# A hybrid decoder layer on one core: root steps and products of some recurrent heads moved from GpSimd to VectorE

## The chip, the core and the metric

The kernel runs on one core of a Trainium2 chip. The metric is the device time of one execution in microseconds (us). A core has TensorE (PE in the profile: matrix products and transposes; PEld is its loading of weights), VectorE (DVE), ScalarE (ACT), GpSimd (POOL) and SyncE (SP, which here only issues DMAs). Each engine works through its own queue in order; an instruction that waits for another engine holds everything behind it in its queue.

## The reference

One decoder layer over 512 tokens of width 1024, in float32. What matters here is the first part of it, the recurrent half of the token mixing (RWKV-7, 8 heads of 64, which the kernel handles as 4 pairs):

```python
kk = k * k_k
kk = kk / max(norm(kk), 1e-12)                   # root 1, per head and token
k  = k * (1 + (a - 1) * k_a)
# per token: S = S*w + (S @ -kk) x (kk*a) + v x k;   y = S @ r
y = (y - mean(y)) * rsqrt(var(y) + 64e-5)        # root 2, per head and token
y = y * gn_w + gn_b
y = (y + sum(r * k * r_k) * v) * g
```

Beside it stands an attention over blocks of 256 keys (8 heads). Then come an output projection with a LayerNorm, a router that picks 2 of 32 experts, the experts, and a second LayerNorm.

## The kernel before

The kernel goes through four stages: the recurrent heads with all input projections (to about 345 us of the profiled execution), attention with the output projection (to about 430), routing (to about 490), and the experts, whose weights are streamed from memory, with the last LayerNorm.

In the first stage the heads come in pairs, `hp` = 0 to 3 (called first to fourth head below, as the code has one index for a pair). For each pair there are four functions. `feat(hp)` makes three projections (k, r, v) and from them the tiles AR and BK, with root 1 on the way. `pre(hp)` turns eight chunks of 64 tokens into the factors of a recurrence over chunks; in its middle stands a loop of 15 steps of three small VectorE instructions (lines 578 to 580), and behind it the mask products Z (line 611), each of which a VectorE transpose (line 630) and then TensorE wait for. `chain(hp)` runs the recurrence over the chunks. `gnorm(hp)` normalises the result, with root 2 (`rsqrt`), a transpose by TensorE of the spread-out root, a scaling (line 700), an addition (line 701) and the gate (line 704). The projections of the next pair and of the attention (24 matrix products each) are TensorE's filling work between these. Each projection needs its weights split into a high and a low part: ScalarE makes the high part (line 336), GpSimd or for a few of them VectorE the low part (line 337). Line 229 is the helper for every matrix product (`mm`), line 232 the one for every transpose on TensorE (`tp`).

The order in each engine's queue in this stage isn't written by hand: a planner sorts the instructions by the priority given in the code and by its own durations, and it is run anew for each version of the kernel.

Both roots go through one helper, `rsqrt`, on tiles of 128 x 8: VectorE makes a first guess (lines 239 and 240), GpSimd halves the argument (line 241) and makes three Newton steps of four instructions (lines 243 to 246), and ScalarE spreads the result to 128 x 512 (line 247). TensorE's transposes (line 232) wait for that.

Of the kernel before, what the change touches and what calls it, by code (L numbers as in the profile page):

```python
# [13 lines left out]
OP = mybir.AluOpType  # L14
# [171 lines left out]
def layer(ctx: ExitStack, tc: tile.TileContext, xT, xt, wb, wad, pc, wla, al, gl, cst, cst2, cst3, abias, wout,  # L186
          lnp, lnt, wr, br, wex, out):
    nc = tc.nc
    PE, V, S, P, SP = nc.tensor, nc.vector, nc.scalar, nc.gpsimd, nc.sync
# [44 lines left out]
    def bc(ap, n):  # L234
        return ap[:, None, :].to_broadcast([128, n, ap.shape[1]])

    def rsqrt(out, y, x, t):

        V.tensor_scalar(t.bitcast(I32), x.bitcast(I32), 1, None, op0=OP.logical_shift_right)
        V.tensor_scalar(y.bitcast(I32), t.bitcast(I32), -1.0, float(0x5F3759DF), op0=OP.mult, op1=OP.add)  # L240
        P.tensor_scalar(x, x, -0.5, None, op0=OP.mult)
        for j in range(3):
            P.tensor_tensor(t, y, y, op=OP.mult)
            P.tensor_tensor(t, t, x, op=OP.mult)
            P.tensor_scalar(t, t, 1.5, None, op0=OP.add)
            P.tensor_tensor(y, t, y, op=OP.mult)
        S.activation(v3(out, 8), y[:, :, None].to_broadcast([128, 8, 64]), AF.Copy)  # L247
# [151 lines left out]
    def feat(hp, fill=()):  # L399
# [4 lines left out]
        d = st[hp] = {}  # L404
        c8 = lambda t: v3(t, 8)
        k, kks, kkn, k2, sig = (T(512, A[3]) for _ in range(5))
# [3 lines left out]
        AR, BKt, bv = d["AR"], d["BK"], d["bv"] = slots[hp % 2]  # L410
        sig3 = v3(sig.f, 4)
        ar, bk = c8(AR.f), c8(BKt.f)
        E3, Ei3 = v3(E.f, 8), v3(Ei.f, 8)
# [19 lines left out]
            mm(pn[:, 2 * i:2 * i + 2], kks.f[:, 128 * i:128 * i + 128], cc("hsel")[:, 0:2], start=(i == 0))  # L433
        nx = T(24)
        V.tensor_scalar(nx.f[:, 0:8], pn[:, 0:8], 1e-24, None, op0=OP.max)
        rsqrt(kkn.f, nx.f[:, 8:16], nx.f[:, 0:8], nx.f[:, 16:24])
        pi = bank(LB)
        for i in range(4):
            tp(pi[:, 128 * i:128 * i + 128], kkn.f[:, 128 * i:128 * i + 128])
# [12 lines left out]
        P.tensor_scalar(k2.f, th.f, -1.0, HA.f[:, 4 + hp:5 + hp], op0=OP.add, op1=OP.mult)  # L452
        V.scalar_tensor_tensor(k2.f, k2.f, 1.0, k.f, op0=OP.add, op1=OP.mult)
        V.scalar_tensor_tensor(bk[:, :, 0:64], c8(kkn.f), 0.5, Ei3[:, :, 1:65], op0=OP.mult, op1=OP.mult)
        P.tensor_tensor(bk[:, :, 64:128], c8(k2.f), Ei3[:, :, 1:65], op=OP.mult)
        V.tensor_tensor(fac.f[:, 8 * hp:8 * hp + 7], E3[:, 0:7, 64], Ei3[:, 1:8, 0], op=OP.mult)
        at("fg", hp)
        ps = bank(PB)
# [2 lines left out]
        r = kks  # L461
        shift_evac(ps, r.f, f"muR{hp}")
        more()
        P.tensor_tensor(ar[:, :, 0:64], c8(r.f), E3[:, :, 1:65], op=OP.mult)  # L464
        V.scalar_tensor_tensor(r.f, r.f, pcol(f"rk{hp}"), k2.f, op0=OP.mult, op1=OP.mult)
        at("fi", hp)
        ps = bank(PB)
# [68 lines left out]
    def pre(hp, W, RB):  # L536
        d = st[hp]
# [4 lines left out]
        for w in range(2):  # L542
            P.memset(bd[w][0:64, :, 64:128], 0.0)
            P.memset(bd[w][64:128, :, 0:64], 0.0)
            for h in range(2):
                q = slice(64 * h, 64 * h + 64)
# [10 lines left out]
        for g in range(2):  # L557
# [9 lines left out]
            for dst, src, m in ((t16, pa4, "m16"), (t32, pa4, "m32"), (akt, pk4, "mstr")):  # L567
# [3 lines left out]
                                op=OP.mult)  # L571
# [35 lines left out]
        for g in range(2):  # L607
            cs = slice(4 * g, 4 * g + 4)
            Z, X, Y, WB = T(512, *W), T(512, *W), T(512, *W), T(1024, *W)
            bufs += [Z, X, Y, WB]  # L610
            P.tensor_tensor(Z.f.rearrange("p (c q t) -> p c q t", c=4, q=8),
                            z3[:, cs, None, :].to_broadcast([128, 4, 8, 16]),
                            cc("bm16")[:, None, :, None].to_broadcast([128, 4, 8, 16]), op=OP.mult)
            wb5 = WB.f.rearrange("p (c w h j) -> p c w h j", c=4, w=2, h=2)
            P.memset(wb5[0:64, :, :, 1, :], 0.0)
            P.memset(wb5[64:128, :, :, 0, :], 0.0)
            G.append((g, cs, Z, X, Y, v3(Z.f, 4), v3(X.f, 4), v3(Y.f, 4), wb5, v4(WB.f, 4, 2)))
# [62 lines left out]
    def gnorm(hp, GB):  # L680
        d = st[hp]
# [9 lines left out]
            mm(pv[:, 2 * i:2 * i + 2], sq.f[:, 128 * i:128 * i + 128], cc("hsel")[:, 2:4], start=(i == 0))  # L691
        nx = T(24)
        V.tensor_scalar(nx.f[:, 0:8], pv[:, 0:8], 64e-5, None, op0=OP.add)
        rsqrt(sq.f, nx.f[:, 8:16], nx.f[:, 0:8], nx.f[:, 16:24])
        at("gb", hp)
        pi = bank(GB)
        for i in range(4):
            tp(pi[:, 128 * i:128 * i + 128], sq.f[:, 128 * i:128 * i + 128])
        nx.free()
        V.scalar_tensor_tensor(yc.f, yc.f, pcol(f"gw{hp}"), pi, op0=OP.mult, op1=OP.mult)  # L700
        P.tensor_tensor(yc.f, yc.f, d["bv"].f, op=OP.add)
        pg = bank(GB)
        mm(pg, Gl.f[0:96, 128 * hp:128 * hp + 128], SG.f[0:96])
        V.tensor_tensor(Y, yc.f, pg, op=OP.mult)
# [905 lines left out]
```

## Time and profile before

| | |
|---|---|
| three runs | 754.66, 757.50 and 757.62 us, median 757.5 |
| profiled execution: its time, its span | 756.99 us, 754.9 us |
| busy share of the span | PE 87%, DVE 48%, ACT 36%, POOL 28% |
| mean granted TensorE clock | 0.931 of full |

The span reaches from the first to the last instruction. Busy shares are means over all stages. A granted clock of 1.00 is TensorE's 2.4 GHz, 0.50 its 1.2 GHz. All times of rows are us from the span's start.

### The profile page before, as it was taken

Reading aid. Unit: us, or ns where it says so; the run is one execution under the profiler, and the core shown is the slowest. Engines: PE = TensorE matmul, PEld = TensorE weight load, DVE = VectorE, ACT = ScalarE, POOL = GpSimd, SP = SyncE. Lnnn points to the kernel's source line nnn. Section 1 sums busy time; section 2 is a strip of 40 time slices with the busy share of each in tenths; the row PEclk is TensorE's granted clock in tenths of the full one; section 3 lists DMA queues with packets and bytes.
Section 4 is the critical chain, followed back from the end, with each engine's and each line's share of the span. In section 5 each row is a group of like instructions: output and inputs, shape, how many; then the busy total and the mean of one; then the engine's idle time right before and its main releaser. Section 6 shows DMA issues by size and latency. Waiting matters only on the chain.

```text
span 754.9 us, 9697 instructions
## 1 busy us (share of the span) xinstructions
PE 660.1 (87%) x3420; PEld 416.7 (55%) x3420; DVE 359.1 (48%) x1091; ACT 273.0 (36%) x581; POOL 211.4 (28%) x302
## 2 busy tenths in 40 slices
PE   8879999889998997979999997599999897779780
PEld 3757887688777876845675676333334232323240
DVE  4277258415841585236445587922121121103975
ACT  4344543544274444536424532223131131101330
POOL 4233553445345533110000041721111111101432
PEclk9979999999999999998989997899999998988985
DMA  9611011001100110465440467499999999999503
GB/s 327 233 56 57 29 56 57 28 29 57 57 29 28 53 46 1 140 238 173 156 158 38 153 237 282 165 358 420 423 426 423 425 421 425 425 417 410 227 2 115
DMA packets 28484, 147.18 MB, mean 195 GB/s; under 512 B 5114, under 2 KB 5626, under 8 KB 20493
## 3 DMA queue, kind: packets, MB, share of 16 engines
q1 hardware_dynamic: 23676, 134.61, 45.5%
q0 software_dynamic: 4608, 11.62, 3.9%
q8 instruction: 29, 0.48, 0.3%
q10 hardware_dynamic: 144, 0.26, 0.1%
q14 instruction: 27, 0.21, 0.1%
HBM read 138.38 MB, written 15.36 MB: 204 GB/s over the span
## 4 chain that ended last, share of the span: by engine, by line
PE 30%; DMA 18%; DVE 8%; POOL 2%; issue 1%; ACT 0%; SPq 0%; DVEq 0%; POOLq 0%; ACTq 0%
PE bank L229 26%; DMA b<-in_wex 17%; PE bank L232 4%; DVE a L147 2%; DVE base L1375 1%; DMA b<-hdram,base 1%; DVE x L1075 1%; DVE base L1204 1%; DVE base L147 1%; POOL base L1007 0%; DVE base L778 0%; POOL base L1012 0%; DVE a L1431 0%; DVE x L1226 0%; POOL x L1086 0%
## 5 line engine op out<-in xcount | busy, mean ns | idle before, releaser
L229 PE MATMUL bank<-a,b 128*128 128x512 f32 (+2 forms) x1112 | 308.7, 467 | 14.9 <-DMA a<-in_wex 12.3
L229 PEld LDWEIGHTS bank<-a,b 128*128 128x128 f32 (+1 forms) x1112 | 159.7, 177 | 94.7 <-issue 47.2
L229 PE MATMUL bank<-b,base 128*64 128x512 f32 (+1 forms) x412 | 93.4, 497 | 8.6 <-DMA b<-in_wex 6.9
L229 PE MATMUL bank<-a,base 128*64 128x512 f32 (+3 forms) x308 | 73.5, 560 | 1.2 <-DMA a<-in_wex 0.8
L337 POOL TENSOR_TENSOR b<-b,b 128x1024 fp32r<-128x1024 f32 x22 | 52.3, 2376 | 73.6 <-ACT b L336 64.6
L229 PEld LDWEIGHTS bank<-b,base 128*64 128x64 f32 (+1 forms) x412 | 42.4, 161 | 49.5 <-issue 34.2
L229 PE MATMUL bank<-a 128*128 128x128 f32 (+6 forms) x264 | 62.7, 370 | 7.2 <-ACT a L627 3.8
L1209 DVE SCALAR_TENSOR_TENSOR base<-bank,base 128x256 f32<-128x256 f32 x16 | 7.7, 483 | 116.9 <-ACT base L1208 116.9
L1208 ACT ACTIVATE base<-bank 128x256 f32<-128x256 f32 x16 | 6.1, 384 | 121.8 <-PE bank L229 121.8
L229 PEld LDWEIGHTS bank<-a 128*128 128x128 f32 (+2 forms) x264 | 37.9, 200 | 20.6 <-issue 6.1
L229 PEld LDWEIGHTS bank<-a,base 128*64 128x64 f32 (+2 forms) x308 | 27.3, 140 | 39.0 <-issue 27.2
L229 PE MATMUL bank<-a,a 128*128 128x128 f32 (+2 forms) x200 | 43.2, 334 | 2.1 <-POOL a L464 2.1
L232 PE MATMUL bank<-base,a 128*128 128x128 f32 x152 | 33.1, 298 | 9.5 <-ACT a L247 7.8
L229 PEld LDWEIGHTS bank<-a,a 128*128 128x128 f32 x200 | 33.2, 202 | 9.5 <-issue 3.7
L229 PE MATMUL bank<-base 128*128 128x36 f32 (+4 forms) x136 | 30.2, 365 | 6.7 <-DVE base L1040 3.3
L336 ACT ACTIVATE b<-b 128x1024 fp32r<-128x1024 f32 x25 | 26.3, 1057 | 26.1 <-PE bank L229 18.7
L232 PE MATMUL bank<-base 128*128 128x128 f32 x156 | 31.1, 302 | 5.1 <-DVE base L1209 3.9
L232 PEld LDWEIGHTS bank<-base 128*128 128x128 f32 x156 | 19.0, 149 | 27.9 <-issue 16.3
L232 PEld LDWEIGHTS bank<-base,a 128*128 128x128 f32 x152 | 19.3, 148 | 22.4 <-ACT a L247 8.9
L229 PE MATMUL bank<-b,a 128*128 128x128 f32 x192 | 31.4, 276 | 0.2 <-DVE a L633 0.2
L229 PEld LDWEIGHTS bank<-b,a 128*128 128x128 f32 x192 | 29.9, 191 | 2.7 <-DVE a L633 0.4
L1298 POOL DMA_INDIRECT ydram<-x,base x13 | 13.1, 1008 | 63.9 <-ACT base L1214 34.6
(302 smaller groups left out, 960.5 us busy)
## 6 DMA issues: line engine op xcount, KB each, us to landing
a<-in_wex SPq DMA_DIRECT2D x28, 2048.0 KB, 24.0
b<-in_wex SPq DMA_DIRECT2D x30, 1024.0 KB, 26.4
b<-in_wb SPq DMA_DIRECT2D x25, 512.0 KB, 3.3
a<-in_wex SPq DMA_DIRECT2D x16, 512.0 KB, 15.7
ydram<-base SPq DMA_DIRECT2D x1, 4096.0 KB, 15.1
a<-ydram POOLq DMA_DIRECT2D x4, 1024.0 KB, 16.0
x<-in_wout SPq DMA_DIRECT2D x6, 512.0 KB, 4.3
a<-in_xT SPq DMA_DIRECT2D x8, 256.0 KB, 5.0
```

The lines of the kernel that those rows point to most:

```text
L147: ins = f(*args, **kw)
L229: return inorder(PE.matmul(o, l, r, start=start, stop=stop, skip_group_check=True))
L232: return inorder(PE.transpose(o, i, late("ident")))
L336: S.activation(hi.f, raw.f, AF.Copy)
L337: (V if 0 < k < 4 else P).tensor_tensor(lo.f, raw.f, hi.g, op=OP.subtract)
L1075: V.scalar_tensor_tensor(ww[:, :, 0], ww[:, :, 0], gs, og, op0=OP.mult, op1=OP.mult)
L1204: V.scalar_tensor_tensor(hb[:, i, ns], hb[:, i, ns], 1.0, pc_, op0=OP.mult, op1=OP.add, accum_out=SUM.f[:, 2 * i + n:2 * i + n + 1] if p = ...
L1208: S.activation(hd.f, ph[:, 0:256], AF.Silu)
L1209: V.scalar_tensor_tensor(hd.f, ph[:, 256:512], GT.f[:, p:p + 1], hd.f, op0=OP.mult, op1=OP.mult)
L1298: P.indirect_dma_start(out=ydram, out_offset=bass.IndirectOffsetOnAxis(ap=IDY.i[:, p:p + 1], axis=0), in_=Y.g, in_offset=None, bounds_chec ...
L1375: E.tensor_tensor(h, h, RT[i].f[:, 1024 * r + 512 * n:1024 * r + 512 * n + 512], op=OP.add)
```

## The change

In `rsqrt` a new flag, `alone`, puts the whole root on VectorE: it drops the halving instruction and makes each Newton step of three instructions instead of four, one `tensor_tensor` and two `scalar_tensor_tensor`. The flag is set for root 1 of the first head (hp = 0) and for root 2 of the third and the fourth head (hp = 2, 3). Five products and additions change from GpSimd to VectorE in some heads: the second half of BK and the r part of AR in the first head, the mask products Z in the first and the fourth head (two each), and the addition of line 701 in the first three heads. All else stays as it was.

```diff
-    def rsqrt(out, y, x, t):
+    def rsqrt(out, y, x, t, alone=False):
         V.tensor_scalar(t.bitcast(I32), x.bitcast(I32), 1, None, op0=OP.logical_shift_right)
         V.tensor_scalar(y.bitcast(I32), t.bitcast(I32), -1.0, float(0x5F3759DF), op0=OP.mult, op1=OP.add)
-        P.tensor_scalar(x, x, -0.5, None, op0=OP.mult)
-        for j in range(3):
+        if alone:
+            for j in range(3):
+                V.tensor_tensor(t, y, y, op=OP.mult)
+                V.scalar_tensor_tensor(t, t, -0.5, x, op0=OP.mult, op1=OP.mult)
+                V.scalar_tensor_tensor(y, t, 1.5, y, op0=OP.add, op1=OP.mult)
+        else:
+            P.tensor_scalar(x, x, -0.5, None, op0=OP.mult)
+        for j in range(0 if alone else 3):
             P.tensor_tensor(t, y, y, op=OP.mult)
...
-        rsqrt(kkn.f, nx.f[:, 8:16], nx.f[:, 0:8], nx.f[:, 16:24])
+        rsqrt(kkn.f, nx.f[:, 8:16], nx.f[:, 0:8], nx.f[:, 16:24], hp == 0)
...
-        P.tensor_tensor(bk[:, :, 64:128], c8(k2.f), Ei3[:, :, 1:65], op=OP.mult)
+        (P if hp else V).tensor_tensor(bk[:, :, 64:128], c8(k2.f), Ei3[:, :, 1:65], op=OP.mult)
...
-        P.tensor_tensor(ar[:, :, 0:64], c8(r.f), E3[:, :, 1:65], op=OP.mult)
+        (P if hp else V).tensor_tensor(ar[:, :, 0:64], c8(r.f), E3[:, :, 1:65], op=OP.mult)
...
-            P.tensor_tensor(Z.f.rearrange("p (c q t) -> p c q t", c=4, q=8),
+            (P if 0 < hp < 3 else V).tensor_tensor(Z.f.rearrange("p (c q t) -> p c q t", c=4, q=8),
...
-        rsqrt(sq.f, nx.f[:, 8:16], nx.f[:, 0:8], nx.f[:, 16:24])
+        rsqrt(sq.f, nx.f[:, 8:16], nx.f[:, 0:8], nx.f[:, 16:24], hp > 1)
...
-        P.tensor_tensor(yc.f, yc.f, d["bv"].f, op=OP.add)
+        (P if hp < 3 else V).tensor_tensor(yc.f, yc.f, d["bv"].f, op=OP.add)
```

## Rows read from the trace of the kernel before

**Rows 1.** Stretches: length, then busy of PE, PEld, DVE, ACT, POOL; PEclk, DMA share.
```profile
36.30:39.60 3.30, 3.22 (x11) 2.46 (x11) 0.88 (x2) 0.73 (x2) 0.00 (x0) 0.50 0.00 0
60.00:270.00 210.00, 197.48 (x1165) 162.73 (x1165) 108.10 (x340) 98.68 (x190) 96.56 (x149) 0.98 0.13 43
285.50:288.70 3.20, 2.58 (x9) 2.30 (x10) 1.40 (x4) 3.09 (x8) 0.61 (x1) 0.50 0.00 0
336.70:346.80 10.10, 7.90 (x31) 4.93 (x31) 4.77 (x12) 4.39 (x11) 2.34 (x7) 0.50 0.57 194
...
550.00:700.00 150.00, 130.03 (x551) 47.88 (x548) 31.12 (x65) 29.10 (x65) 20.23 (x22) 0.93 1.01 421
```

**Rows 2.** TensorE's waits, 0 to 345: total us, times, longest.
```profile
PE bank L232 <- ACT a L247: 7.8, 3, 3.7
...
PE bank L232 <- ACT b L247: 2.6, 1, 2.6
```

**Rows 3.** Timeline, root 1 of the first head: start, us, [idle before <-releaser].
```profile
31.65 0.17 DVE L239 TENSOR_SCALAR base<-base 128x8 int32<-128x8 int32 x1
...
31.86 0.17 DVE L240 TENSOR_SCALAR base<-base 128x8 int32<-128x8 int32 x1
...
35.57 0.63 ACT L247 ACTIVATE a<-base 128x512 f32<-128x512 f32 x1 [2.42 <-POOL base L246]
...
36.25 1.12 PE L232 MATMUL bank<-base,a 128*128 128x128 f32 x4 [1.97 <-ACT a L247]
```

**Rows 4.** Timeline, products of the first head and what follows them.
```profile
40.13 0.68 DVE L450 SCALAR_TENSOR_TENSOR a<-a 128x512 f32<-128x512 f32 x1
...
40.30 1.55 POOL L455 TENSOR_TENSOR a<-a 128x512 f32<-128x512 f32 x1 [4.76 <-ACT a L448]
...
43.56 1.22 PE L229 MATMUL bank<-a,a 128*128 128x128 f32 x4 [2.13 <-POOL a L464]
...
44.21 1.10 DVE L454 SCALAR_TENSOR_TENSOR a<-a 128x512 f32<-128x512 f32 x1
...
52.22 6.89 PE L229 MATMUL bank<-a,b 128*128 128x512 f32 x22 [2.52 <-DVE b L337]
```

**Rows 5.** Timeline, root 2 of the third head beside the fourth head's loop.
```profile
278.02 0.17 DVE L240 TENSOR_SCALAR base<-base 128x8 int32<-128x8 int32 x1
...
279.89 2.37 POOL L337 TENSOR_TENSOR b<-b,b 128x1024 fp32r<-128x1024 f32 x1
279.99 2.37 DVE L579 TENSOR_TENSOR base<-base 128x80 f32<-128x80 f32 x1
...
282.44 1.63 POOL L477 TENSOR_SCALAR b<-b,base 128x512 f32<-128x512 f32 x1
...
282.97 0.30 DVE L579 TENSOR_TENSOR base<-base 128x72 f32<-128x72 f32 x1
...
285.43 0.63 ACT L247 ACTIVATE a<-base 128x512 f32<-128x512 f32 x1 [3.76 <-POOL base L246]
...
287.26 0.75 DVE L700 SCALAR_TENSOR_TENSOR a<-a,base,bank 128x512 f32<-128x512 f32 x1 [2.12 <-PE bank L232]
...
288.19 1.23 DVE L579 TENSOR_TENSOR base<-base 128x48 f32<-128x48 f32 x1
```

**Rows 6.** Timeline, mask products of the fourth head.
```profile
293.59 1.07 POOL L611 TENSOR_TENSOR a<-base,x 128x512 f32<-128x512 f32 x1 [4.23 <-DVE base L580]
...
296.87 0.71 DVE L630 STREAM_TRANSPOSE base<-a 128x512 f32<-128x512 f32 x1 [1.47 <-POOL a L611]
...
297.73 1.13 PE L229 MATMUL bank<-base,a 128*128 128x128 f32 x8 [0.64 <-DVE base L630]
```

**Rows 7.** Timeline, root 2 of the fourth head.
```profile
334.34 0.88 DVE L521 TENSOR_SCALAR a<-a,base 128x512 f32<-128x512 f32 x2
...
338.22 0.63 ACT L247 ACTIVATE b<-base 128x512 f32<-128x512 f32 x1 [2.98 <-POOL base L246]
```

**Rows 8.** The chain that ended last, in order of time: start, us, what.
```profile
553.69 30.05 DMA b<-in_wex
```

## The prediction

> **What bounds the kernel now.** I read the granted clock and busy shares by stretch first, then the chain that ended last, TensorE's waits, and the timeline around each edited line. Three things are to be seen.
>
> The chain ends in the expert weights: from 553.7 on it runs through loads of some 30 us each [rows 8], and from 550 to 700 the DMA engines are full, share 1.01 [rows 1]. But before 553.7 the chain runs through TensorE and the engines that it waits for, back into the recurrent stage. Each expert load starts when its buffer comes free, so what TensorE saves before 553 moves the whole stream forward, one for one.
>
> In the recurrent stage TensorE is nearly full: of the 210 us from 60 to 270 it is busy 197.5 [rows 1]. Its work there doesn't change. What can be won is idle time of TensorE, and what its clock loses after idle time.
>
> Third, the idle time sits where the change works. TensorE waits 7.8 us in three places for a spread root of the first three heads, and 2.6 us for that of the fourth [rows 2]. Two of these four places, the first (1.97, [rows 3]) and the longest (3.7), and the fourth head's 2.6 are roots that the change moves; the remaining 2.1 us belong to a root that stays. TensorE's low clock level, 0.50 or 1.2 GHz, is granted in 36.3 to 39.6, 285.5 to 288.7 and 336.7 to 346.8 [rows 1]: each time with or just after one of these three waits. In the 210 us from 60 on, over which 12.5 us of idle time are spread, the mean is 0.98 of 2.4 GHz.
>
> **The change part by part.** I cost the parts as time by which TensorE gets ahead.
>
> *Root 1, first head.* VectorE's two guess instructions start 0.21 us apart [rows 3], at 0.17 us each. No row shows a `tensor_tensor` or `scalar_tensor_tensor` of this root on VectorE; for 128 x 8 I take the same spacing. Nine steps from 32.03 (end of line 240) end at 32.03 + 9 x 0.21 = 33.92, and ScalarE's spreading starts at about 34.0 instead of 35.57 [rows 3]: 1.6 us. What stands next in VectorE's queue, the product of line 441, needs the root itself, so nothing is held up. Bounds: 1.2 (steps of 0.25) and 1.97, the whole wait. The wait left would be 0.4 us, too little, by the long stretch from 60 on, to cost the clock. In 36.3 to 39.6 TensorE is busy 3.22 us at 1.2 GHz [rows 1], which is 1.61 at 2.4; since steps of other engines stand between its pieces I take 1.1 of these 1.6 us, bounds 0 and 1.6.
>
> *Products of BK and AR, first head.* On GpSimd the first takes 1.55 us, and TensorE waits 2.13 us for the second [rows 4]. On VectorE such a product takes 0.68 (line 450). VectorE's queue then holds seven instructions from 40.13 on: six of about 0.7 and one small one, 4.4 us together, where today it reaches the end of line 454 at 44.21 + 1.10 = 45.31, 5.2 us after 40.13. So the last one comes 0.75 us sooner. What follows it is a ScalarE copy, the split of the weights and TensorE's wait at 52.22 (2.52, [rows 4]); that wait moves forward and does not shrink. I take 0.75; bounds 0 (GpSimd's parallel work was worth as much) and 2.1 (the planner puts the two products first, and the wait of 2.13 goes).
>
> *Mask products, first head.* VectorE gets two more products and its transposes no longer wait for GpSimd. TensorE has projection work there and no wait that names them; cost and gain nothing. Without that cover the gain is some 0.4 us each, as in the fourth head below.
>
> *Root 2, third head.* Today the root starts after line 240 (278.19) and its spreading at 285.43 [rows 5], 7.2 us for work that costs 3.5 in the first head: GpSimd's split of 2.37 us and line 477 of 1.63 stand in the middle of it. On VectorE the steps share the queue with the fourth head's loop. With one loop instruction between two steps (0.42 us a step) four are done by 279.89; then the split runs and a two-input VectorE instruction stands still (line 579: 2.37 instead of 0.30, [rows 5]) until 282.3; five more steps end at 284.4. With the steps first, eight are done before the split and the ninth at 282.5. So the gain is 1.0 to 2.9 us; I take 1.7. The lower bound is a loss of 0.8, if line 477 holds it up too. Queued behind a held step are the loop's instructions, and TensorE waits for the loop's end.
>
> *The loop and Z, fourth head.* The loop's end decides when Z starts (293.59, [rows 6]). VectorE gets 9 x 0.21 = 1.9 us of steps and 0.68 for line 701. It loses an idle 2.12 before line 700, which waits for the root's transposes, and the 0.9 us that line 579 stands still behind line 701 on GpSimd (1.23 against 0.30, [rows 5]). Net -0.5: the loop ends no later. Then two products and two transposes follow each other on VectorE, 2 x 0.68 + 2 x 0.71 = 2.8 us, and end near 296.4 where today the second ends at 297.58. TensorE waits 0.64 us for it [rows 6], and that is what I take; bounds +0.64 and -1.7 (the idle time before line 700 stays and the loop is longer by that).
>
> *Additions of line 701, heads one to three.* 0.68 on VectorE instead of GpSimd. Only the gate of line 704 follows, whose result nobody needs before attention. Nothing, hidden under TensorE's projections; uncovered, 0.68 each.
>
> *Root 2, fourth head.* Its spreading starts at 338.22 [rows 7]; the guess is done just before 334.34. On VectorE nine steps are 1.9 us, and the attention's two scalings, 0.88 together [rows 7], with a few smaller instructions come between: the end is near 337.2, 1.0 us earlier. Bounds 0 (all of the attention's work goes first) and 2.1 (none of it). From 336.7 to 346.8 TensorE is busy 7.90 us at 1.2 GHz [rows 1], so this fall costs up to 3.95. The other two falls, after waits of 1.97 and 3.7, cost 1.6 and 1.3. If the shorter wait leaves a fall of that size the gain is 2.5; I take half of it, 1.2, with bounds 0 and 3.95.
>
> No DMA moves from one queue to another, and no SyncE instruction is added.
>
> A rule of the Trainium skill speaks against the change. By "SBUF — State Buffer", section "Who interferes with whom", a VectorE instruction with two inputs in SBUF and a GpSimd instruction that reads SBUF exclude each other for the whole length of the one that started first. All nine steps and all moved products have two such inputs. The trace agrees for the split (2.37 us of line 579), and not fully for line 477, beside which line 579 took 0.30 us [rows 5]. By the rule the root of the third head would come near 286.2, and the sum would be that of the second rival.
>
> **The sum.** 1.6 + 1.1 + 0.75 + 1.7 + 0.64 + 1.0 + 1.2 = 8.0 us. The profiled execution took 756.99 us, 0.5 below the median of the three runs and inside their spread of 3 us: 756.99 - 8.0 = 749.0.
>
> **The rivals.**
>
> *The clock stays up.* The shorter waits no longer let the clock fall, in the third head (2.58 us busy at 1.2 GHz, 1.3 back) and in the fourth (3.95 instead of 1.2), and the two products come first (2.1 instead of 0.75). 5.4 more: 743.6. For it: the unmoved root's wait of 2.1 us lies in a stretch whose mean is 0.98. Against: the first fall came with a wait of only 1.97.
>
> *GpSimd holds VectorE.* Line 477 stops the steps and the loop like the split does: the five steps left start at 282.44 + 1.63 = 284.07 and end at 286.2, a term of -0.8, and the loop ends 1.6 later. 1.6 + 1.1 + 0.75 - 0.8 - 1.6 + 1.0 + 1.2 = 3.2: 753.8. For it the 2.37, against it the 0.30 [rows 5].
>
> *The gain ends at the weights.* If the stream of expert weights starts no sooner, its full engines hide all: 757.0. Against it: the chain is TensorE's before 553.7.
>
> *The queues are written anew, for the worse.* The planner's order depends on its own durations, and the moved instructions change them from the first head on. In 60 to 270, where hardly anything is moved, TensorE idles 210 - 197.48 = 12.5 us [rows 1]; an order that puts a transpose or a weight split behind a waiting instruction adds there. It decides as soon as it adds more than the 8.0 won; doubled, it gives 757 - 8.0 + 12.5 = 761.5. For it: today's order already has a split in the middle of a root. Against: TensorE is 94% full there, and most parts of the order hang on priorities.
>
> **How the numbers follow.** Half of a per cent, 3.8 us, is about what a measurement of this kernel can tell from no change: below 753.2 is faster, above 760.8 slower. Chances: the forecast (745.5 to 753) 0.50, clock stays up 0.16, GpSimd holds VectorE 0.14, weights 0.08, queues for the worse 0.12. Faster: 0.50, 0.16 and a third of the third case, 0.70; slower: most of the last, 0.10; same: the rest, 0.20. The range runs from 743.0, just below the clock's case, to 757.0, which takes in the weights' case and leaves out the last one and the far end of the first.
>
> **What would show it.** The first spreading near 34.0 with a wait below 0.5; no 0.50 clock at 36 to 40; root 2 of the third head in under 6.5 us; second transpose of Z less than 3 us after the loop's end; the last root in under 3.2 us; the first full-rate expert load some 8 us earlier. I am wrong if TensorE's idle time before 345 falls by less than 4 us, if a two-input VectorE step regularly takes over 0.4 us, or if new waits appear between 60 and 270.

## The result and the profile after

The changed kernel takes 745.5 us (median of 4 runs, 743.6 to 747.0) against 756.7 for the kernel before (4 runs beside it, 754.7 to 757.6): a ratio of 0.9848, 95% interval 0.981 to 0.9886. Forecast were 749.0 us, range 743 to 757. On 756.5 us, about the median of the kernel before in all the comparisons here, the ratio is a gain of 11.5 us (8.6 to 14.4), where the sum had 8.0. Ratios here leave out runs over 1.5% above the fastest of their kernel (three of e1_head1's ten, one of e2_root3's), medians take in all. The changed kernel's profiled execution took 747.0 us with a span of 745.1 and a mean clock of 0.939.

One sentence ahead of the prediction is wrong, and the diff beside it is right: the condition `P if hp < 3 else V` moves the addition to VectorE in the fourth head alone. In the first three heads it stays on GpSimd. Two terms of the prediction rest on that misreading; they come below.

In the changed kernel the lines behind `rsqrt` stand six lower: the spreading is line 253, the split 343, the loop 584 to 586, Z 617, the addition 707. VectorE's root steps are lines 243 to 245. Busy time by engine, from the page of the changed kernel:

```profile
PE 657.2 (88%) x3420; PEld 413.3 (55%) x3420; DVE 359.8 (48%) x1125; ACT 272.9 (37%) x581; POOL 195.0 (26%) x256
```

GpSimd has 46 instructions fewer than before, VectorE 34 more, and both kernels have 3,420 matrix products and transposes on TensorE. So the start of the k-th of them can be compared in both traces: the lead of the changed kernel, with idle time between TensorE's instructions and time at the low clock in the same stretch. Idle time of the first head is counted from 26 us on here and below, since the waits for the first loads, near 6 us, differ by about 1 us from trace to trace.

| stretch of before (us) | lead won (profiled) | forecast | idle time saved | low clock saved |
|---|---|---|---|---|
| 0 to 60: first head | 5.0 | 1.6 + 1.1 + 0.75 | 4.2 | 3.4 |
| 60 to 256 | -1.4 | 0 | -0.9 | -3.4 |
| 256 to 303: third head's root, fourth head's loop and Z | 3.6 | 1.7 + 0.64 | 1.8 | 3.4 |
| 303 to 375: last root | 2.5 | 1.0 + 1.2 | 2.0 | 6.8 |
| 375 to 724 | 0.1 | 0 | about 0 | 3.4 |
| together | 9.8 | 8.0 | | |

The lead is 9.7 at 375 us, 9.7 at 404 and 9.8 at 724: what TensorE saves before the end of attention reaches the end of the kernel. Two pieces of the chain that ended last in the changed kernel say the same; its first long wait for expert weights starts at 544.02 where [rows 8] have 553.69.

```profile
275.66 2.27 DVE base L245
...
544.02 29.92 DMA b<-in_wex
```

The first of the two lines is a root step of VectorE, an instruction on 128 x 8, that was for 2.27 us what everything waited for. The section on the reasons comes back to it. The stretches of [rows 1] in the changed kernel (length, busy time of PE, PEld, DVE, ACT and POOL, granted clock, DMA share), with two of the stretches in which its clock was low (to 345 us three others, of 3.4 us each, start at 132.3, 156.1 and 200.5):

```profile
36.30:39.60 3.30, 1.87 (x12) 1.49 (x12) 2.83 (x5) 1.56 (x4) 0.00 (x0) 1.00 0.00 0
39.90:46.70 6.80, 5.51 (x19) 4.47 (x20) 4.36 (x6) 4.49 (x7) 2.67 (x2) 0.51 0.05 13
60.00:270.00 210.00, 196.63 (x1161) 161.97 (x1160) 107.14 (x341) 98.93 (x191) 92.73 (x145) 0.98 0.12 41
285.50:288.70 3.20, 2.60 (x16) 1.91 (x14) 2.87 (x14) 1.87 (x5) 0.74 (x2) 1.00 0.00 0
330.10:333.50 3.40, 3.33 (x21) 2.27 (x21) 0.98 (x7) 2.09 (x6) 0.00 (x0) 0.52 0.71 188
336.70:346.80 10.10, 10.10 (x48) 5.24 (x47) 8.10 (x20) 5.77 (x15) 0.00 (x0) 1.00 0.66 220
```

At the times of the three low stretches of [rows 1] the clock is now 1.00. But one low stretch stands at 39.9, 3.6 us behind the place of the first and twice as long, and one at 330.1, a third as long as that at 336.7 and over much the same work, which now comes earlier. That at 285.5 has no successor. TensorE's waits for the spread roots, to 345 us, were 7.8 in three and 2.6 in one place [rows 2]; now:

```profile
PE bank L232 <- ACT a L253: 4.3, 2, 2.2
```

The two are 2.11 us for a root that was not moved and 2.20 us for the moved root of the third head.

**First head.** The timeline of the changed kernel, to be held against [rows 3, 4]:

```profile
32.40 0.17 DVE L240 TENSOR_SCALAR base<-base 128x8 int32<-128x8 int32 x1
32.61 0.17 DVE L243 TENSOR_TENSOR base<-base 128x8 f32<-128x8 f32 x1
32.81 0.17 DVE L244 SCALAR_TENSOR_TENSOR base<-base 128x8 f32<-128x8 f32 x1
...
34.22 0.17 DVE L245 SCALAR_TENSOR_TENSOR base<-base 128x8 f32<-128x8 f32 x1
34.41 0.63 ACT L253 ACTIVATE a<-base 128x512 f32<-128x512 f32 x1 [0.72 <-DVE base L245]
35.10 0.66 PE L232 MATMUL bank<-base,a 128*128 128x128 f32 x4
...
37.84 0.69 DVE L456 SCALAR_TENSOR_TENSOR a<-a 128x512 f32<-128x512 f32 x1
...
41.36 0.74 DVE L471 SCALAR_TENSOR_TENSOR a<-a,base 128x512 f32<-128x512 f32 x1
...
44.25 1.22 DVE L343 TENSOR_TENSOR b<-b,b 128x1024 fp32r<-128x1024 f32 x1
...
44.85 2.84 POOL L343 TENSOR_TENSOR b<-b,b 128x1024 fp32r<-128x1024 f32 x1 [3.95 <-ACT b L342]
```

The steps follow each other at 0.20 us. From line 240 to the spreading it is 2.01 us instead of 3.71, and the transposes don't wait; one matrix product more stands ahead of them, and a wait of 0.46 us comes behind them, at 36.67. The seven instructions from line 456 to line 471 take 4.26 us. Then come two weight splits side by side, VectorE's first: it takes 1.22 us, and the next projection has no wait. Before, GpSimd's came first, and VectorE's took 3.26, as the instructions of line 337 in the kernel before show from 44 to 54 us (shortest/median/longest ns, first and last start):

```profile
L337 POOL TENSOR_TENSOR b<-b,b x1: 2357/2357/2357, 48.7 to 48.7; 128x1024 fp32r<-128x1024 f32 x1
L337 DVE TENSOR_TENSOR b<-b,b x1: 3255/3255/3255, 48.9 to 48.9; 128x1024 fp32r<-128x1024 f32 x1
```

That is where the wait of 2.52 us at 52.22 [rows 4] came from: VectorE's split stood for 3.26 - 1.22 = 2.0 us beside GpSimd's.

**Third head's root, fourth head's loop**, again the timeline of the changed kernel, beside [rows 5, 6]:

```profile
273.85 0.17 DVE L240 TENSOR_SCALAR base<-base 128x8 int32<-128x8 int32 x1
...
275.47 2.44 POOL L343 TENSOR_TENSOR b<-b,b 128x1024 fp32r<-128x1024 f32 x1 [5.95 <-ACT b L342]
275.58 2.35 DVE L245 SCALAR_TENSOR_TENSOR base<-base 128x8 f32<-128x8 f32 x1
...
278.64 1.56 POOL L483 TENSOR_SCALAR b<-b,base 128x512 f32<-128x512 f32 x1 [0.74 <-DVE base L243]
278.82 0.59 DVE L585 TENSOR_TENSOR base<-base 128x72 f32<-128x72 f32 x1
...
279.58 0.63 ACT L253 ACTIVATE a<-base 128x512 f32<-128x512 f32 x1 [1.99 <-DVE base L245]
280.26 1.09 PE L232 MATMUL bank<-base,a 128*128 128x128 f32 x8 [2.20 <-ACT a L253]
282.20 1.26 POOL L707 TENSOR_TENSOR a<-a 128x512 f32<-128x512 f32 x1 [2.00 <-DVE a L706]
282.27 1.26 DVE L586 TENSOR_TENSOR base<-base 128x48 f32<-128x48 f32 x1
...
287.42 1.29 DVE L617 TENSOR_TENSOR a<-base,x 128x512 f32<-128x512 f32 x2
...
289.39 1.16 PE L229 MATMUL bank<-a 128*128 128x128 f32 x8 [0.39 <-DVE a L636]
```

From line 240 to the spreading it is 5.73 us instead of 7.41, with one step, which usually takes 0.16 us, standing 2.35 beside the split. TensorE still waits 2.20.

**Last root**, beside [rows 7]:

```profile
327.51 0.17 DVE L240 TENSOR_SCALAR base<-base 128x8 int32<-128x8 int32 x1
...
330.73 2.30 PE L229 MATMUL bank<-a,b 128*64 128x128 f32 x14
331.33 0.62 ACT L253 ACTIVATE b<-base 128x512 f32<-128x512 f32 x1
...
332.96 0.96 PE L232 MATMUL bank<-base,b 128*128 128x128 f32 x4
```

From line 240 to the spreading it is 3.82 us instead of 4.15; line 240 of the kernel before is

```profile
334.07 0.17 DVE L240 TENSOR_SCALAR base<-base 128x8 int32<-128x8 int32 x1
```

### The profile page after: what moved, and what is told of

It is laid out like the page before. It is cut to its first block, busy times and chain, and to the rows that moved or that the text cites. A ratio compares the mean times of both kernels' runs of the same rounds, so it can differ in the third digit from the quotient of the medians.

```text
span 745.1 us, 9680 instructions
## 1 busy us (share of the span) xinstructions
PE 657.2 (88%) x3420; PEld 413.3 (55%) x3420; DVE 359.8 (48%) x1125; ACT 272.9 (37%) x581; POOL 195.0 (26%) x256
## 4 chain that ended last, share of the span: by engine, by line
PE 35%; DMA 18%; DVE 11%; POOL 2%; issue 1%; ACT 1%; SPq 0%; DVEq 0%; POOLq 0%; ACTq 0%
PE bank L229 31%; DMA b<-in_wex 17%; PE bank L232 4%; DVE a L147 2%; DVE base L1381 1%; DMA b<-hdram,base 1%; DVE x L1081 1%; DVE base L1210 1%; DVE base L147 1%; DVE base L586 0%; POOL base L1013 0%; DVE base L585 0%; DVE base L784 0%; DVE base L245 0%; DVE base L584 0%
## 5 line engine op out<-in xcount | busy, mean ns | idle before, releaser
L229 PEld LDWEIGHTS bank<-a,b 128*128 128x128 f32 (+1 forms) x1112 | 159.1, 177 | 92.2 <-issue 49.8
L229 PEld LDWEIGHTS bank<-a 128*128 128x128 f32 (+2 forms) x264 | 36.4, 190 | 21.1 <-issue 7.2
L601 ACT ACTIVATE b<-bank 64x256 f32<-64x256 f32 x64 | 24.3, 379 | 16.4 <-PE bank L232 15.5
```

The source lines that it names most:

```text
L229: return inorder(PE.matmul(o, l, r, start=start, stop=stop, skip_group_check=True))
L601: S.activation(dst[qd, cs, o_:o_ + 64], pt4[q, :, 64 * h:64 * h + 64], AF.Copy)
```

## Experiments

Gains are (1 - ratio) x 756.5 us, with the interval worked out in the same way. The ratio is not the quotient of the two medians: medians alone give 3.3 us for e1_head1, 4.6 for e5_prods, 2.1 for e9_split and 17.6 for e10_split23, so a difference of 2 us between two gains is not to be read. Diffs are against the changed kernel, where not said otherwise.

| run | what | median (us) | ratio, 95% interval | gain (us) |
|---|---|---|---|---|
| changed kernel | | 745.5 | 0.9848, 0.981 to 0.9886 | 11.5 (8.6 to 14.4) |
| e1_head1 | first head's parts alone | 753.2 | 0.9928, 0.9887 to 0.997 | 5.4 (2.3 to 8.5) |
| e8_h1root | first head's root alone | 753.0 | 0.9968, 0.9938 to 0.9997 | 2.4 (0.2 to 4.7) |
| e2_root3 | third head's root alone | 750.9 | 0.9935, 0.9909 to 0.9961 | 4.9 (3.0 to 6.9) |
| e3_root4 | fourth head's root alone | 750.6 | 0.9928, 0.9901 to 0.9956 | 5.4 (3.3 to 7.5) |
| e4_roots | the three roots | 749.1 | 0.9899, 0.9858 to 0.994 | 7.6 (4.5 to 10.7) |
| e5_prods | products and addition alone | 751.9 | 0.992, 0.9891 to 0.9948 | 6.1 (3.9 to 8.2) |
| e6_fill | before, last wait filled | 754.8 | 0.9971, 0.994 to 1.0003 | 2.2 (-0.2 to 4.5) |
| e9_split | before, one more split on VectorE | 754.0 | 0.9991, 0.9962 to 1.0021 | 0.7 (-1.6 to 2.9) |
| e7_all | changed, all eight roots | 742.6 | 0.9804, 0.9763 to 0.9846 | 14.8 (11.7 to 17.9) |
| e10_split23 | changed, one more split on VectorE | 738.4 | 0.9753, 0.971 to 0.9795 | 18.7 (15.5 to 21.9) |

**e1_head1: the first head's parts alone.**
```diff
-            (P if 0 < hp < 3 else V).tensor_tensor(Z.f.rearrange(...
+            (V if hp == 0 else P).tensor_tensor(Z.f.rearrange(...
-        rsqrt(sq.f, nx.f[:, 8:16], nx.f[:, 0:8], nx.f[:, 16:24], hp > 1)
+        rsqrt(sq.f, nx.f[:, 8:16], nx.f[:, 0:8], nx.f[:, 16:24], False)
-        (P if hp < 3 else V).tensor_tensor(yc.f, yc.f, d["bv"].f, op=OP.add)
+        P.tensor_tensor(yc.f, yc.f, d["bv"].f, op=OP.add)
```


> Only the first head's parts (root 1, both products, the mask products of that head). If the parts add up in place, TensorE is 5.4 us ahead of the kernel before at about 60 us, as in the changed kernel, and 3.5 to 5.5 ahead at the end: 751.5 to 753.5 for a kernel before at 757. If the gain of the first head hangs on the order of the whole plan, it is under 3 us at 60 us and the end is within 2 us of the kernel before.

A gain of 5.4 us. In its trace the lead is 5.8 at 60 us and 4.1 at the end; idle time to 60 us fell by 4.2, as in the whole change. The forecast had 3.45 for these parts, inside the interval but well below the middle.

**e8_h1root: of these, the root alone** (BK, AR, Z, the addition and both second roots back as before).
```diff
-        (P if hp else V).tensor_tensor(bk[:, :, 64:128], c8(k2.f), Ei3[:, :, 1:65], op=OP.mult)
+        P.tensor_tensor(bk[:, :, 64:128], c8(k2.f), Ei3[:, :, 1:65], op=OP.mult)
-        (P if hp else V).tensor_tensor(ar[:, :, 0:64], c8(r.f), E3[:, :, 1:65], op=OP.mult)
+        P.tensor_tensor(ar[:, :, 0:64], c8(r.f), E3[:, :, 1:65], op=OP.mult)
```


> Only the nine Newton steps of the first head's first root move. The prediction's terms: 1.6 for the root and 1.1 for the clock, 2.7 us, 753.7 from 756.4, with the wait of 2.52 us at 52 us still there. Rival, that the order of the two engines around the fifth weight split decides in the first head and that the steps alone turn it: the wait at 52 us is gone as in the whole change, and the gain is that of all the first head's parts, 3.3 to 5.4 us (751 to 753). Second rival: the steps alone hide behind something else late at 36 us, and it gives under 1 us (756).

The gain of 2.4 us is what the terms gave (2.7). But their picture of the wait at 52 us is wrong: in TensorE's timeline the projection behind the split has

```profile
49.20 5.28 PE L229 MATMUL bank<-a,b 128*128 128x512 f32 x22 [0.30 <-DVE b L343]
```

0.30 us instead of 2.52. The rival was right about the wait; its price (3.3 to 5.4) is above the measured gain, though inside the interval from 3.3 to 4.7. In e4_roots, with the same instructions up to the third head, it is 1.64:

```profile
49.48 5.28 PE L229 MATMUL bank<-a,b 128*128 128x512 f32 x22 [1.64 <-DVE b L343]
```

There GpSimd's split started at 46.0 and VectorE's, at 46.8, took 2.63 us; in e8_h1root they started at 45.7 and 47.4 and VectorE's took 1.71. VectorE's split ends 1.1 us behind GpSimd's in both, as in the kernel before, so the wait is what is left of GpSimd's split when VectorE's comes up. Idle time to 60 us fell by 3.8, nearly as in the whole change. Further on this trace loses it again: a VectorE loop instruction at 55.44 stands 2.51 us beside a GpSimd split, TensorE waits 2.09 at 60.19, and from 60 to 237 us the clock is low for 10.2 us more than in the kernel before. The profiled execution took 757.7 us, where the median is 753.0, so this trace is no measure of the root's gain.

**e2_root3 and e3_root4: a second root alone** (all products, the addition and the first root back as before).
```diff
-        rsqrt(sq.f, nx.f[:, 8:16], nx.f[:, 0:8], nx.f[:, 16:24], hp > 1)
+        rsqrt(sq.f, nx.f[:, 8:16], nx.f[:, 0:8], nx.f[:, 16:24], hp == 2)   # e3_root4: hp == 3
```


> Only root 2 of the third head on VectorE. Forecast's step: the wait of 3.7 us becomes about 2.2 and TensorE is 1.7 to 2.3 us ahead by 300 us, time 755 for 757 before. Rival that GpSimd holds VectorE: the wait stays above 3.3 and the time is within 1 us of before. If the fall of the clock at 285 goes as well, 1.3 us more.

> Only root 2 of the fourth head on VectorE. If wait and clock are both won: the wait of 2.6 us is under 0.5, the half-clock stretch of 10 us is 3.4 us long, gain 3.5 us, 753.5 for 757 before. If only the wait counts: gain 1.0 to 1.5. If the clock stretch has nothing to do with that wait it stays 10 us long.

They gained 4.9 and 5.4 us, where the terms were 1.7 and 1.0 + 1.2; both intervals leave the terms out. In the stretch from 273 to 301 us e2_root3 won 3.0 us (idle time 1.2, low clock 3.4), with the same held step (line 245 at 278.46, 2.34 us beside line 343) and the same wait of 2.20 as the whole change. In the stretch from 322 to 357 e3_root4 won 6.8 (idle time 2.1, low clock 10.2); the clock there, from 326 to 350, is 1.00:

```profile
326.00:350.00 24.00, 22.13 (x121) 12.35 (x119) 18.93 (x68) 16.74 (x41) 1.48 (x2) 1.00 0.80 284
```

Whether the low stretch at 336.7 [rows 1] hangs on the last root, all traces tell together. With this root on GpSimd it is 6.8 to 13.7 us long (seven profiles, without e6_fill); with it on VectorE it is absent in e3_root4 and e10_split23, 3.4 in both profiles of the changed kernel, 6.9 in e7_all, and in e4_roots as long as before:

```profile
328.30:338.50 10.20, 10.03 (x36) 6.38 (x37) 5.05 (x16) 4.79 (x11) 2.25 (x1) 0.50 0.60 249
```

So it tends to be shorter, and the root alone does not decide. The third head's low stretch is clearer: it stands in all eight profiles with that root on GpSimd (starting between 281.3 and 289.2) and in one of the six with it on VectorE (e7_all, 275.4).

The two traces also have a lead of over 2 us at 60 us, where their instructions are those of the kernel before in the same order: in e2_root3 it is 6.8 us less of low clock, in e3_root4 1.8 us less idle time. A single trace measures a part to no better than that.

**e5_prods: products and addition alone.**
```diff
-        rsqrt(kkn.f, nx.f[:, 8:16], nx.f[:, 0:8], nx.f[:, 16:24], hp == 0)
+        rsqrt(kkn.f, nx.f[:, 8:16], nx.f[:, 0:8], nx.f[:, 16:24], False)
-        rsqrt(sq.f, nx.f[:, 8:16], nx.f[:, 0:8], nx.f[:, 16:24], hp > 1)
+        rsqrt(sq.f, nx.f[:, 8:16], nx.f[:, 0:8], nx.f[:, 16:24], False)
```


> Only the products and the addition on VectorE, all roots as before. Forecast's step: the first head's products give 0.75 us, the mask products 0.6, end 755.5 for 757 before. Rival: the products let VectorE start its weight split before GpSimd's, so the wait of 2.5 us at 52 us and the fall of the clock after it go, and 3 us or more are won before 60 us.

A gain of 6.1 us, where the terms for these edits were 0.75 + 0.64. From 26 to 60 us idle time fell by 2.6: VectorE's split ran first (47.4, 1.21 us) and GpSimd's beside it took 3.15, so the wait at 52 us is gone. Around Z, 273 to 301, idle time fell by 0.9.

**e4_roots: the three roots without the products** (BK, AR, Z and the addition back on GpSimd).
```diff
-            (P if 0 < hp < 3 else V).tensor_tensor(Z.f.rearrange(...
+            P.tensor_tensor(Z.f.rearrange(...
```


> Only the three roots move (first root of the first head, second root of the third and fourth); all products and the addition stay on GpSimd. The prediction's terms for the roots with the clock give 1.6 + 1.1 + 1.7 + 1.0 + 1.2 = 6.6 us: 749.8 from a median of 756.4, and 4.9 more when the products go too, so less than the whole change. Rival, from the pieces: the second roots of the third and the fourth head alone gave 5.5 and 5.8 us, so the roots alone should give all that the whole change gives (11 us, some 745.5), and the products are worth nothing beside them. Between them, 747 to 749, the parts overlap: each alone takes away waits that another part would have taken away as well.

7.6 us, near the terms (6.6) and away from the rival's 11. So the products bring 11.5 - 7.6 = 3.9 beside the roots. The three roots alone add up to 2.4 + 4.9 + 5.4 = 12.7 and together give 7.6. With half-widths of 2.2, 2.0, 2.1 and 3.1, which make 4.8 taken as independent, that is just outside of chance: each part alone seems to win something that another would also have won. In the first head that is the wait at 52 us, which the root alone takes down to 0.30 and the products alone remove. For the three roots the runs don't settle it.

**c1_before and c2_after: the kernel before and the changed kernel, unchanged, profiled once more.**

> The kernel before, unchanged, profiled a second time. The experiments so far hold the same instructions as the kernel before up to about 265 us, yet two of them were 2.2 and 2.5 us ahead of it at 60 us, with TensorE's half-clock stretches at other places. If these places change from execution to execution, this profile differs from the first by 1 to 3 us at some landmarks of the recurrent stage, with half-clock stretches elsewhere and waits that differ in pairs (a slower TensorE waits less). If they are fixed by the instructions, it repeats the first within 0.3 us at each landmark.

> The changed kernel, unchanged, profiled a second time. If the half-clock stretches wander, the lead over the kernel before at 60 and at 237 us is not 5.1 and 3.7 again but differs by 1 to 3 us, and the gains in idle time (4.2 us in the first head, 1.8 in the third, 2.3 in the last) stay within 0.7.

These were for the places of the low clock; the two executions took 760.6 and 744.3 us. To 300 us it was low, in the first profile of the kernel before, from 36.3, 43.1, 53.3, 159.1, 230.8 and 285.4 on; in the second from 43.4, 63.9, 139.0, 162.9, 207.2 and 289.2. Most of the early places wander with the same instructions, the later ones come back: 336.6 and 391.2 against 340.4 and 398.4 (10.3 and 6.9 us long against 13.6 and 3.4), and in the changed kernel 330.1 and 381.3 against 327.0 and 378.2. Against its first profile the second of the kernel before is 1.7 us ahead at 60 us, 3.2 behind at 256 and 5.1 at 375, where 1 to 3 were expected. The changed kernel's lead is 6.8 at 60 and at 237 us this time, while the idle time that it saves repeats within 0.1 us (4.2 in the first head, 1.8 and 2.0 in the third and fourth head's stretches).

Part of what differs between executions is again GpSimd beside VectorE. In the second profile of the kernel before

```profile
58.31 2.39 POOL L337 TENSOR_TENSOR b<-b,b 128x1024 fp32r<-128x1024 f32 x1 [7.36 <-PE bank L229]
58.32 2.51 DVE L580 TENSOR_TENSOR base<-base 128x104 f32<-128x104 f32 x1
...
63.07 1.31 PE L229 MATMUL bank<-a 128*128 128x512 f32 x2 [1.85 <-DVE a L476]
```

a loop step stands for 2.51 us, with a split that started 0.01 us before it, and TensorE's wait of 1.85 us is new. In the first profile the same split started only at 60.05, and the step reads

```profile
58.43 0.27 DVE L580 TENSOR_TENSOR base<-base 128x104 f32<-128x104 f32 x1
```

**e6_fill: the kernel before with TensorE busy in the last root's wait.** Twenty small products (40 instructions of TensorE) into a tile that is overwritten before anyone reads it.
```diff
+        if hp == 3:
+            for i in range(20):
+                mm(pi[:, 0:128], cc("cen"), Y[:, 0:128])
         for i in range(4):
             tp(pi[:, 128 * i:128 * i + 128], sq.f[:, 128 * i:128 * i + 128])
```


> The kernel before, with 20 extra small products on TensorE placed while it waits for the last root; their result is overwritten unread. If the half-clock stretch of 10 us behind that wait comes from TensorE standing idle, it is 3.4 us long or gone and the time is 2 to 4 us lower, though no wait is shorter. If the wait alone is what the change won there, the time stays within 1 us or rises by up to 1.

The root is as late as before, the wait is filled, and the clock stays up where [rows 1] have 0.50:

```profile
334.32 4.73 PE L229 MATMUL bank<-base 128*128 128x128 f32 x40
```
```profile
336.70:346.80 10.10, 9.58 (x68) 7.07 (x66) 6.48 (x14) 5.55 (x12) 2.42 (x7) 1.00 0.67 237
```

In the seven other profiles with this root on GpSimd the clock does fall. So idle time in front is what makes it fall here. The time is 2.2 us lower (-0.2 to 4.5) with nothing else won, so what the clock gives back here is not told from nothing; the sum had 1.2 with a bound of 3.95, of which the larger end is not ruled out. The filling itself, 4.73 us, outlasts the wait of 2.57, so this is a lower figure.

**e9_split: the kernel before with the fifth split on VectorE too.**
```diff
-        (V if 0 < k < 4 else P).tensor_tensor(lo.f, raw.f, hi.g, op=OP.subtract)
+        (V if 0 < k < 5 else P).tensor_tensor(lo.f, raw.f, hi.g, op=OP.subtract)
```


> The kernel before, with one more weight split (the fifth) on VectorE, so that in the first head no split on GpSimd can hold VectorE's. If the wait of 2.5 us at 52 us came from VectorE's split standing still behind GpSimd's (3.25 us instead of 1.22), it falls below 1 us and the first head gains 1.5 to 2.5 us. If it came from ScalarE's lateness, it stays at 2 or more and nothing is won.

GpSimd's split beside VectorE's is gone, and VectorE's takes 1.22 us. The wait of 2.52 at 52.22 shrinks to 0.46:

```profile
50.30 3.92 PE L229 MATMUL bank<-a,b 128*128 128x512 f32 x16 [0.46 <-DVE b L337]
```

From 26 to 60 us idle time fell by 1.9. That the wait was the one split standing beside the other is shown. The time is 0.7 us less (-1.6 to 2.9): 1.9 fits, no gain fits too.

**e7_all: all eight roots on VectorE.**
```diff
-        rsqrt(kkn.f, nx.f[:, 8:16], nx.f[:, 0:8], nx.f[:, 16:24], hp == 0)
+        rsqrt(kkn.f, nx.f[:, 8:16], nx.f[:, 0:8], nx.f[:, 16:24], True)
-        rsqrt(sq.f, nx.f[:, 8:16], nx.f[:, 0:8], nx.f[:, 16:24], hp > 1)
+        rsqrt(sq.f, nx.f[:, 8:16], nx.f[:, 0:8], nx.f[:, 16:24], True)
```


> The changed kernel with the Newton steps of all eight roots on VectorE. In the changed kernel TensorE still waits 1.54 us at 79.7, 2.11 at 131.7, 2.25 at 154.9, 1.28 at 200.2 and 2.61 at 225.6 us, near the roots that stayed. By the theory that a root on VectorE is 1.5 us shorter wherever TensorE waits for it, three to five of them give 3 to 6 us: 740 to 742.5 from 745.5. Rival: VectorE is already late where the other roots stand (the waits at 225.6 us and others name VectorE, not the spread), and its two-input steps are held by GpSimd's splits for up to 2.4 us; then it is as before within 1.5 us or up to 3 us slower, 744 to 749.

742.6 us, 2.9 less than the changed kernel; the six runs (740.2 to 743.6) and its four (743.6 to 747.0) just touch. TensorE's waits at 131.66 (2.11) and 154.9 (2.25) are gone; one at 125.99 (1.79) takes their place, and the one at 79.67 (1.54) is 2.30 at 77.27. In the stretch from 142 to 237 us it won 5.2 us on the kernel before, with 2.2 us less of idle time and 6.8 less of low clock; elsewhere it gave back some. A root instruction stands 2.2 us beside a split in four places (71.9, 147.6, 217.5 and 269.3), as the rival had it. Both theories hold in part, and the sum is at the lower edge of the first.

**e10_split23: the changed kernel with the split at 275.5 us on VectorE.**
```diff
-        (V if 0 < k < 4 else P).tensor_tensor(lo.f, raw.f, hi.g, op=OP.subtract)
+        (V if 0 < k < 4 or k == 23 else P).tensor_tensor(lo.f, raw.f, hi.g, op=OP.subtract)
```


> The changed kernel with one more weight split (the one that GpSimd ran at 275.5 us for 2.44 us while a root step of VectorE stood 2.35 us beside it) also on VectorE. By the theory that the split holds the third head's root, the root ends 1.1 to 2.4 us earlier (1.2 us of VectorE's own time for the split at most takes the place of 2.35), so 743.2 to 744.5 from 745.5, and no step near 275 us takes over 1.3 us. Rival: the split on VectorE is queued ahead of the root and starts as late as its load, so the root waits for it all the same, and the time stays within 0.7 us of 745.5.

738.4 us (736.6 to 741.0): the fastest, some 7 below the changed kernel (7.2 by the two ratios, 6.4 by the medians, each against the kernel before beside it), and no run of the one within the other's. The timeline at the third head's root:

```profile
273.18 0.16 DVE L240 TENSOR_SCALAR base<-base 128x8 int32<-128x8 int32 x1
...
274.73 1.23 DVE L343 TENSOR_TENSOR b<-b,b 128x1024 fp32r<-128x1024 f32 x1
...
275.88 0.16 DVE L245 SCALAR_TENSOR_TENSOR base<-base 128x8 f32<-128x8 f32 x1
...
278.10 0.63 ACT L253 ACTIVATE a<-base 128x512 f32<-128x512 f32 x1
```

No step is held. The root takes 4.92 us instead of 5.73, and TensorE's wait of 2.20 behind it is gone: it won 1.7 us more than the changed kernel from 256 to 303. That much was expected. But the root is shorter by only 0.8. The planner also wrote TensorE's queue anew: three projection products now stand between four other transposes (277.33) and the root's, where the changed kernel has all eight together.

```profile
277.75 0.94 PE L229 MATMUL bank<-a,b 128*128 128x512 f32 x3
278.78 0.66 PE L232 MATMUL bank<-base,a 128*128 128x128 f32 x4
```

The rest was not expected: low clock that is gone, 1.6 us of idle time saved between 303 and 345 us, and some 2.5 us given back behind 404. The changed kernel had a low clock at 330.1 and at 381.3; here, from 320 to 328 and over the products that answer to the second of them, it is 1.00:

```profile
320.00:328.00 8.00, 7.80 (x43) 4.80 (x44) 5.53 (x27) 5.77 (x16) 0.50 (x2) 1.00 0.71 284
352.00:400.00 48.00, 46.44 (x246) 30.33 (x244) 27.31 (x89) 20.95 (x56) 0.00 (x0) 1.00 0.20 77
```

In the changed kernel the second of the two stretches reads:

```profile
381.30:388.10 6.80, 6.80 (x27) 5.57 (x26) 1.91 (x8) 2.47 (x5) 0.00 (x0) 0.51 0.97 389
```

6.80 us busy at the low level are 3.4 at the high one, and the 3.33 at 330.1 are 1.7: together 5.1. The lead over the kernel before is 19.7 us at 404 and 17.4 at the end. Whether the low stretches went with the held step and the wait at 280 us is not shown. This is one profile against two of the changed kernel, and TensorE's queue differs from the changed kernel's in many places from 277.7 to 391.7 us: the rival that this order, and not the end of the hold, won the rest was not tested.

## Why the prediction was right, and where it was not

**What bounds the kernel.** Right: the changed kernel carries its lead of 9.7 us at 404 to the end one for one, and the weights' rival is out. (e9_split and e10_split23 gave back some 2.4 us behind 404.) But the prediction named three low stretches of the clock where its trace has seven to 347 us; those from 43.1 and 53.3, beside the waits of 2.13 and 2.52 us [rows 4], it did not weigh.

**Root 1, first head.** Right: 1.70 us from line 240 to the spreading, term 1.6. The term of 1.1 for the clock there was not won as put: the low stretch moved from 36.3 to 39.9, and in the time of the root alone (2.4 us) the two cannot be told apart.

**Products of the first head: the mis-sized term.** VectorE's seven instructions take 4.26 us instead of 5.2, 0.9 less, so the term's working held. What failed is the step "that wait moves forward and does not shrink": the wait of 2.52 at 52.22 is gone. It was VectorE's split held by a GpSimd split that started 0.2 us sooner; with less work on GpSimd and an earlier projection VectorE's starts first, and then it is GpSimd's that stands longer (2.84 instead of 2.36), for which nobody waits. The split's 3.26 us beside GpSimd's 2.36 could be read in the trace of before, as line 579 was read in [rows 5]; the working took TensorE's wait and left out what its releaser had stood behind. Either part of the change takes it away: in idle time to 60 us the root alone saves 3.8 of the whole change's 4.2 us, the products alone 2.6. In run time the products bring 3.0 us by e1_head1 less e8_h1root, 3.9 by the whole less e4_roots (with Z's) and 6.1 alone (with Z's), each uncertain by 2 to 4 us. The wait is large enough to carry most of the 3.5 us between 8.0 and 11.5, but its share and the clock's can't be told apart.

**Root 2, third head.** Right for the root: 1.68 us (7.41 less 5.73), term 1.7, with the one held step that the working put there (2.35 us). The time won is larger, 3.0 to 6.9 us for the root alone: the low stretch at 285.5 [rows 1] went with it, in five of six profiles, which the sum had left to the clock's rival. In e2_root3's trace the stretch brought 3.0 us; what lies above that in the runs stays open. By the Trainium skill ("SBUF — State Buffer", section "Who interferes with whom") a VectorE instruction with two inputs in SBUF and a GpSimd instruction that reads SBUF exclude each other for the length of the one that started first. The trace agrees for line 245 beside the split and for line 586 beside the addition (1.26 beside 1.26); not fully for line 483, a GpSimd instruction with one tile as its input, beside which line 585 took 0.59 in 1.56. So the rival "GpSimd holds VectorE" is out as it was priced, since line 483 does not stop the steps. The split does hold a step, and in e10_split23 the kernel without that hold, in an order of its own, is 7 us faster; in the place of the hold 1.7 us are won.

**Loop and Z.** The line 701 part is void: the addition stayed on GpSimd in the third head and held the loop for 1.26 us as before. The loop ended with Z's two products and transposes close behind, 2.5 us against 2.8 in the working. TensorE's wait fell from 0.64 to 0.39, where the term took all of it. "Additions in heads one to three" concerned instructions that did not move.

**Root 2, fourth head.** Wrong in mechanism. The root is 3.82 us from line 240 to the spreading, against 338.22 - 334.07 = 4.15. That is 0.33 less, not 1.0, since attention's scalings (line 527, four of 0.41 to 0.48 us) and reductions (line 519) stand between its steps on VectorE. The wait of 2.57 is gone since 14 small attention products, 2.30 us, now stand ahead of the transposes in TensorE's queue. The clock's part, taken at 1.2, is 2.2 (-0.2 to 4.5) by e6_fill, and 3.4 at most by the 6.8 us less of low clock in the profiles; in e4_roots, with the same root moved, it is not there.

**The rivals.** The clock's rival (743.6) came true in part: the low stretch at 285.5 is gone and that at 336.7 a third as long, while the wait of 2.13 before the products of AR and BK is still 1.90, at 41.19. The time lies between it and the forecast, nearer to the rival (1.9 us) than to the forecast (3.5). "Queues written anew, for the worse" can't be told from chance: between 60 and 256 us the first profile lost 1.4 us of lead (0.9 us more idle time, 3.4 more of low clock), the second none, and two executions of the kernel before differ by 5.0 there.

**The signs named.** The first spreading (34.41, with no wait behind it), the root of the third head, Z, the expert load (9.7 us earlier) and TensorE's idle time before 345 us (6.9 less) came out as written. The last root did not (3.82 us, not under 3.2), and the low clock of the first head only moved. Two-input steps took 0.15 to 0.17 us but for the one beside the split.

**Luck.** That the sum came within 3.5 us is in part luck. It missed the wait at 52 us, which was worth up to 2.5, and took too much for the fourth head's root and for Z, 0.7 and 0.4. And the clock moves single executions by more than the 2.3 us that the sum took for it: from 60 to 256 us alone, two executions of the kernel before differ by 6.8 us of low clock, which is 3.4 us of time.

## What to carry to other kernels

Where a TensorE wait names a VectorE instruction, look whether that instruction took its usual time; if it stood beside a GpSimd instruction that started just before, that hold is part of the wait (here 2.0 of 2.52 us, e9_split), and moving either instruction is worth a run. What that run wins is not the price of the hold alone where a planner then sorts the queues anew (here 7 us for one split). A wait taken out of a nearly full TensorE can pay twice, once in its place and again in the clock behind it, as at the third head's root, so size it from a run and not from its length. And two executions of one and the same kernel here differ by up to 5 us over a stretch: time the parts alone over many runs, and don't add them up.

## What was not expected of the hardware

The clock was low from 381.3 to 388.1 with TensorE busy for 6.80 of these 6.80 us and waits of at most 0.7 us since 345 in the changed kernel. Thirteen of the fourteen profiles have such a stretch, of 3.4 or 6.9 us, starting between 377.8 and 398.4; only e10_split23's has none. The same instructions in the same order had it low at 36.3, 43.1 and 53.3 in one execution and at 43.4 and 63.9 in the next. And in one execution of the kernel before, a start 0.01 us behind GpSimd's made a VectorE instruction nine times as long; in the other, where GpSimd's came 1.6 us after it, it took its usual 0.27 us.
